# Tiles of the matmul operands at other offsets modulo 512 bytes, and gating vectors broadcast by DMA, in a two-block diffusion transformer kernel

## The chip, the cores and the metric

The kernel runs on one core of a Trainium2 chip. The metric is the device time of one execution in microseconds (us). A core has TensorE (PE, with its weight load PEld), VectorE (DVE), ScalarE (ACT), GpSimd (POOL) and SyncE (SP, which here only starts DMAs), an on-chip memory of 128 partitions (SBUF), in which a tile lies at the same address in every partition, and accumulators (PSUM) into which TensorE writes.

## The reference

The first block is two layers of a diffusion transformer on two streams of 256 tokens of 1024 columns, a main one and a context one. In short:

```python
mod = (silu_c @ lp["w_mod"] + lp["b_mod"])[:, None, :]
sh1, sc1, gt1, sh2, sc2, gt2 = jnp.split(mod, 6, axis=-1)
...
h = modulate(x, lp["g_norm1"], sh1, sc1)
proj = h @ lp["w_in"]
...
x = x + gt1 * merge_branches(o_mla, o_gqa, o_four, proj[..., GATE_START:], lp)
x = x + gt2 * conv_ffn(modulate(x, lp["g_norm2"], sh2, sc2), lp)
```

`merge_branches` adds a latent attention, a grouped attention and a Fourier mixer under sigmoid gates and multiplies by `w_o`. The context stream does the same with its own `mod` (`gt1`, `gt2` of it are used in layer 0 only). The second block takes the main stream on: swiglu feed-forward parts of 2816 columns (`ffn_wi`, `ffn_wo`), attention mixers with dilated and windowed masks (`a_wqkv`) and an embedding term (`p`). All of it is float32.

`gt1` and `gt2` are the gating vectors: 1024 numbers each, by which every token's row is multiplied. Three pairs of layer and stream use them twice each, so there are six such products.

## The kernel before, in words

**Three products for one.** Each float32 operand of a large product is split into a high half, rounded to the fast format fp32r, and a low half that holds the rest (`split`, L105 to L108: ACT casts the high half at L107, DVE subtracts at L108). `mm3` (L128 to L131) then runs three matmuls into one accumulator: high by high (L129), high by low (L130 or L131, depending on which operand stands first), low by high. A matmul has a stationary operand, 128x128, which PEld loads, and a moving operand, of 256 to 512 columns, which PE streams. The load of the next stationary tile runs beside the streaming of the present matmul. So at any time PE reads two places in the SBUF: the moving tile of one matmul, and the stationary tile of the next.

**Which is which.** Where the names read `mm<-xTh,wh`, the first is the stationary operand's tile for some groups and the moving one for others: weights move past stationary tokens in the token-major products (`L129 mm<-xTh,wh`), and tokens move past stationary weights in the others (`mm<-wh,ckv`, `mm<-wh,yh`, `mm<-wh,xTh`). In the second block each half (j = 0, 1) has 128 tokens, whose tiles `xh`, `xl` (named `x` in the trace), `oh`, `ol` and `gT` are stationary, and the weights move in stretches of 512 or 256 columns.

**Weights.** `load` (L113 to L127) fetches 512 KB into `raw` by an SP DMA and splits it into tiles `wh` and `wl` of 1024 words of 4 bytes per partition. `wsps` is a list of pools from which the pairs are taken in turn.

**Where tiles lie.** A pool gives its tiles out in the order in which they are first asked for, so a tile that nothing uses (`pads`, `pad`, `padk`, `padr`) moves all that stand behind it.

**Modulation vectors.** `w_mod` is summed on DVE chunk by chunk (512 columns) into `acc` tiles, as background pieces among the weight loads. `mod_finish` (L273 to L279) adds the partitions of up to four `acc` by PE (L277) and copies the sums to a row tile by ACT (L279). `mod_columns` (L281 to L289) turns the row into columns by four PE transposes (L287) and adds `b_mod` on DVE (L289), into `mcols`. Chunks 4, 5 are `gt1`, chunks 10, 11 are `gt2`.

**Gating vectors.** `bcast_rows` (L230 to L238) spreads 1024 columns of `mcols` over all partitions: DVE makes a diagonal tile `dg` from the identity and one column (L236, eight times), PE multiplies it with a tile of ones (L237, in plain float32, which the trace shows as two hardware matmuls each), ACT copies the accumulator with a scale, 0.5 or 1 (L238, twice), into `gtb`. It is called ahead of the product with `w_o` in `layer` (L1001) and in the feed-forward part (L1090). DVE multiplies the product by `gtb` at L1010.

A scheduler of the compiler orders each engine's instructions.

Of the kernel before, what the change touches and what calls it, by code (L numbers as in the profile page):

```python
# [11 lines left out]
ALU = mybir.AluOpType  # L12
# [24 lines left out]
FL = (1, 1)  # L37
DS = 1
TC_ARGS = dict(schedule_with_timeline_sim=True)

# [6 lines left out]
def block_kernel(ctx: ExitStack, tc: tile.TileContext, a: dict, out: bass.AP):  # L47
# [9 lines left out]
    xtp = b1.enter_context(tc.tile_pool(name="xtp", bufs=1))  # L57
    pmm = ctx.enter_context(tc.tile_pool(name="pmm", bufs=6, space=PSUM))
    ptp = ctx.enter_context(tc.tile_pool(name="ptp", bufs=2, space=PSUM))
    def mmt():  # L60
# [11 lines left out]

    st.tile([128, 112], F32, name="pads", bufs=1)
    const.tile([128, 80], F32, name="pad")
    ident = const.tile([128, 128], F32, name="ident")
    nc.sync.dma_start(out=ident, in_=a["k_ident"])
    ones = const.tile([128, 128], F32, name="ones")
    dve.memset(ones, 1.0)
# [30 lines left out]

    wsps = [wsp]  # L110
    last_load = [None]

    def load(w, k0, nk, c0, n):  # L113
        raw = wraw.tile([128, CH], F32, tag="raw", name="raw")
        last_load[0] = nc.sync.dma_start(
            out=raw[:, :nk * n].rearrange("p (k c) -> p k c", k=nk),
            in_=w[k0 * 128:(k0 + nk) * 128, c0:c0 + n].rearrange("(k p) c -> p k c", p=128),
        )
        wp = wsps[0]
        wsps.append(wsps.pop(0))  # L120
        h = wp.tile([128, CH], F32R, tag="wh", name="wh")
        lo = wp.tile([128, CH], F32R, tag="wl", name="wl")
# [57 lines left out]
    cols1.tile([128, 40], F32, name="pad1")  # L180
    xbig = [xtp.tile([128, 2 * KD * SEQ], F32R, name=f"xT{i}") for i in "hl"]
    xslot = [0]
# [46 lines left out]

    def bcast_rows(wk, cols, scale, dst):  # L230

        for half in range(2):
            p = tpt()
            for k in range(4):
                dg = wk.tile([128, 128], F32, tag="dg", name="dg", bufs=8)
                dve.tensor_scalar(dg, ident, cols[:, half * 4 + k:half * 4 + k + 1], None, op0=ALU.mult)  # L236
                pe.matmul(p[:, k * 128:(k + 1) * 128], ones, dg, start=True, stop=True)  # L237
            act.activation(dst[:, half * 512:half * 512 + 512], p, ACTF.Copy, scale=scale)  # L238

# [33 lines left out]
    def mod_finish(l, accs):  # L273

        ps = mdt()
        for i, (c, s, acc) in enumerate(accs):
            pe.matmul(ps[32 * i:32 * i + 32, :], ones[:, :32], acc, start=True, stop=True)  # L277
        row, n = accs[0][2], 32 * len(accs)
        act.copy(row[:n], ps[:n])  # L279

    def mod_columns(l, accs):  # L281

        row, n = accs[0][2], 32 * len(accs)
        p2 = mdt()
        pv = p2.rearrange("p (f c) -> p f c", f=4)
        for f in range(4):
            pe.transpose(pv[:, f, :n], row[:n, f * 128:(f + 1) * 128], ident[:n, :n])  # L287
        for i, (c, s, acc) in enumerate(accs):
            dve.tensor_tensor(mcols[l][:, c * 4:c * 4 + 4, s], pv[:, :, 32 * i], bmod[:, l, c * 4:c * 4 + 4], op=ALU.add)  # L289

# [49 lines left out]
    def small(kv, l, q):  # L340

        kv.tile([128, 24], F32, name="padk")
        r = {n: brow(kv, n, a[n][l], a[n].shape[1], q) for n in ("g_ckv", "g_cq", "g_qn_gqa", "g_kn_gqa")}
# [297 lines left out]
    def layer(l, res, qgroups, front):  # L641
# [11 lines left out]
        with ExitStack() as es:  # L653
# [345 lines left out]
            for g in qgroups:  # L999
                gtb[g] = gw_.tile([128, D], F32, tag="gtb", name="gtb")  # L1000
                bcast_rows(gw_, mcols[l][:, 16:24, 1 - g], 0.5, gtb[g])  # L1001
            x2 = new_xT(ng)
# [20 lines left out]
    def conv_ffn(l, res, xT, groups, done):  # L1023
# [6 lines left out]
        with ExitStack() as es:  # L1030
# [5 lines left out]
            for f0, f1 in parts:  # L1036
# [49 lines left out]
                if f0 == 0:  # L1086
                    flush(1 + 3 * l)
                    for g in groups:
                        gtb[g] = fw.tile([128, D], F32, tag="gtb", name="gtb")
                        bcast_rows(fw, mcols[l][:, 40:48, 1 - g], 1.0, gtb[g])  # L1090
                rate, bg_rate[0] = bg_rate[0], R3
# [86 lines left out]
    rg = ctx.enter_context(tc.tile_pool(name="rg", bufs=1))  # L1178
    rg.tile([128, 48], F32, name="padr")
    rope2 = ld(rg, "rope2", a["k_rope2"], [128, 2, 32])  # L1180
    nsink = brow(rg, "nsink", a["b_sink_2"][0], 16)
    dve.tensor_scalar(nsink, nsink, -1.0, 0.0, op0=ALU.mult, op1=ALU.add)
    loaded, gains = {}, {}
    chain = {"end": [], "n": 0}

    def w2t(name, shape=(128, 512), dt=F32):
# [24 lines left out]
    def pre_norm(j, i, n):  # L1211

        g = gain(j, i, n)
        with tc.high_priority(100):
            xT = tuple(rg.tile([128, KD, 128], F32R, tag=f"x{p}{j}", name="x") for p in "hl")
            for hf, sl in enumerate(halves()):
# [62 lines left out]
    def ffn2(j, i, n):  # L1279
# [5 lines left out]
        for c in range(6):  # L1285
# [4 lines left out]
            if c == 0:  # L1290
                t = rg.tile([128, 6144], F32R, tag=f"R{j}", name="gT")[:, :2 * FT * 128].rearrange("p (z f c) -> p z f c", z=2, f=FT)
                gT = (t[:, 0], t[:, 1])
# [35 lines left out]
    def mixer(j, i):  # L1328
# [27 lines left out]
        qT = v3(R, 4608, nqT)  # L1356
        oT = tuple(rg.tile([128, 8, 128], F32R, tag=f"o{p}{j}", name="oT") for p in "hl")

# [263 lines left out]
```

## Time and profile before

| what | value |
|---|---|
| time, median of 3 runs | 2495.92 us (2492.79 to 2496.34) |
| the profiled execution's own time | 2496.4 us |
| its span, first to last instruction | 2494.6 us |
| TensorE's mean granted clock | 0.993 of full speed |
| PE busy | 2420.9 us, 97% of the span |
| PEld, DVE, ACT, POOL busy | 2021.0, 1601.6, 1238.8, 161.1 us |

A matmul's busy time in the trace reaches into the next one's, since matmuls are pipelined. What counts for the end is the distance from one start to the next, called the pitch below, read from the timeline. Full speed of TensorE is 2.4 GHz, one column of a fast-format matmul per cycle: 512 columns take 213.3 ns, 256 take 106.7 ns, and the rest of the pitch is what is lost between two matmuls.

### The profile page before, as it was taken

The page shows a single profiled execution, that of the slowest core. Times are in us where ns is not written, and L with a number is a line of the kernel's source. Part 1 is how long each engine was busy: PE and PEld are TensorE (multiplying, and loading weights), DVE is VectorE, ACT ScalarE, POOL GpSimd, SP SyncE. Part 2 cuts the span into 40 slices and gives each one's busy share as a digit, 9 for nine tenths or more (in the row PEclk, how much of TensorE's full clock was granted, in tenths as well). Part 3 has the DMA queues.
Part 4 walks back from the last instruction along what each step waited for, and adds up shares of the span by engine and source line. Part 5 has one row for each costly group of instructions (what it writes and reads, how often), then busy time and mean ns, then how long its engine had stood idle before and what let it go on. Part 6 is the DMA issues. An engine that isn't in the chain of part 4 may idle for free.

```text
span 2494.6 us, 34647 instructions
## 1 busy us (share of the span) xinstructions
PE 2420.9 (97%) x13091; PEld 2021.0 (81%) x13091; DVE 1601.6 (64%) x2609; ACT 1238.8 (50%) x2044; POOL 161.1 (6%) x291
## 2 busy tenths in 40 slices
PE   7999999999999989999999999999999999999998
PEld 6885788788887878699899788789788788777886
DVE  4457666758877667767786555656654755666555
ACT  4567432344324346744565444556544644475444
POOL 3320000000000025000000000100000100110001
PEclk9999999999999999999999999999999999999999
DMA  7220255424454435157566665662665565525653
GB/s 264 85 64 28 78 171 162 151 82 142 136 177 135 159 97 184 42 187 236 160 182 214 189 186 185 194 186 81 194 186 195 180 187 186 193 86 176 187 186 114
DMA packets 236613, 388.32 MB, mean 156 GB/s; under 512 B 14621, under 2 KB 122045, under 8 KB 236445
## 3 DMA queue, kind: packets, MB, share of 16 engines
q1 hardware_dynamic: 235581, 384.14, 49.1%
q0 software_dynamic: 864, 1.96, 0.3%
q8 instruction: 103, 1.69, 0.3%
q14 instruction: 65, 0.53, 0.1%
HBM read 383.95 MB, written 1.05 MB: 154 GB/s over the span
## 4 chain that ended last, share of the span: by engine, by line
PE 85%; DVE 6%; ACT 3%; DMA 3%; issue 1%; POOL 1%; SPq 0%; DVEq 0%; POOLq 0%; ACTq 0%
PE mm L129 25%; PE mm L131 25%; PE mm L130 25%; DMA raw<-in_w_mod_dram 2%; PE mm L581 2%; PE mm L1423 1%; PE tp L502 1%; ACT p L596 1%; DVE acc L271 1%; DVE wl L108 1%; PE mm L1454 1%; PE tp L1323 1%; PE tp L1300 1%; PE mm L626 1%; DVE p L604 1%
## 5 line engine op out<-in xcount | busy, mean ns | idle before, releaser
L108 DVE TENSOR_TENSOR wl<-raw,wh 128x1024 fp32r<-128x1024 f32 (+2 forms) x612 | 738.7, 1211 | 490.2 <-ACT wh L107 468.2
L107 ACT CAST wh<-raw 128x1024 fp32r<-128x1024 f32 (+2 forms) x612 | 635.2, 1043 | 701.9 <-PE mm L131 470.5
L131 PE MATMUL mm<-wh,x 128*128 128x512 f32 (+1 forms) x1072 | 389.6, 371 | 1.0 <-DVE x L1225 1.0
L130 PE MATMUL mm<-wl,x 128*128 128x512 f32 (+1 forms) x1072 | 386.8, 370 | 0.0
L129 PE MATMUL mm<-wh,x 128*128 128x512 f32 (+1 forms) x1072 | 379.6, 371 | 3.9 <-ACT x L1224 3.5
L129 PE MATMUL mm<-xTh,wh 128*128 128x256 f32 (+1 forms) x1120 | 373.3, 335 | 0.0
L131 PE MATMUL mm<-xTh,wl 128*128 128x256 f32 (+1 forms) x1120 | 372.0, 332 | 0.0
L130 PE MATMUL mm<-xTl,wh 128*128 128x256 f32 (+1 forms) x1120 | 372.0, 332 | 0.0
L129 PEld LDWEIGHTS mm<-wh,x 128*128 128x128 f32 x1072 | 202.0, 189 | 38.9 <-ACT x L1224 6.5
L129 PEld LDWEIGHTS mm<-xTh,wh 128*128 128x128 f32 x1120 | 214.1, 192 | 22.9 <-issue 2.0
L131 PEld LDWEIGHTS mm<-wh,x 128*128 128x128 f32 x1072 | 201.9, 189 | 37.1 <-DVE x L1225 5.2
L131 PEld LDWEIGHTS mm<-xTh,wl 128*128 128x128 f32 x1120 | 213.9, 191 | 20.8 <-issue 0.8
L130 PEld LDWEIGHTS mm<-xTl,wh 128*128 128x128 f32 x1120 | 213.9, 191 | 19.7
L130 PEld LDWEIGHTS mm<-wl,x 128*128 128x128 f32 x1072 | 202.2, 189 | 33.2 <-DVE wl L108 0.3
L271 DVE SCALAR_TENSOR_TENSOR acc<-raw,cT,acc 128x512 f32<-128x512 f32 x224 | 160.3, 746 | 69.7 <-DMA raw<-in_w_mod_dram 68.8
L130 PE MATMUL mm<-wl,gT 128*128 128x512 f32 x352 | 134.9, 391 | 0.0
L131 PE MATMUL mm<-wh,gT 128*128 128x512 f32 x352 | 134.4, 389 | 0.0
L129 PE MATMUL mm<-wh,gT 128*128 128x512 f32 x352 | 116.1, 391 | 0.0
L129 PE MATMUL mm<-wh,gh 128*128 128x512 f32 x264 | 103.7, 394 | 3.1 <-DVE t L1137 3.1
L131 PE MATMUL mm<-wh,gl 128*128 128x512 f32 x264 | 103.6, 392 | 0.0
L130 PE MATMUL mm<-wl,gh 128*128 128x512 f32 x264 | 103.5, 392 | 0.0
L1068 ACT ACTIVATE uc<-mm,cb,cw 128x512 f32<-128x512 f32 (+1 forms) x88 | 58.7, 668 | 72.8 <-PE mm L131 69.9
(328 smaller groups left out, 3783.0 us busy)
## 6 DMA issues: line engine op xcount, KB each, us to landing
raw<-in_ffn_wi_dram SPq DMA_DIRECT2D x176, 512.0 KB, 3.7
raw<-in_w_up_dram SPq DMA_DIRECT2D x88, 512.0 KB, 3.5
raw<-in_ffn_wo_dram SPq DMA_DIRECT2D x88, 512.0 KB, 3.2
raw<-in_w_mod_dram SPq DMA_DIRECT2D x80, 512.0 KB, 4.4
raw<-in_w_in_dram SPq DMA_DIRECT2D x68, 512.0 KB, 4.4
raw<-in_w_down_dram SPq DMA_DIRECT2D x44, 512.0 KB, 4.8
raw<-in_a_wqkv_dram SPq DMA_DIRECT2D x36, 512.0 KB, 4.6
mraw<-in_w_mod_dram SPq DMA_DIRECT2D x16, 512.0 KB, 9.6
```

Source lines behind the costliest of these rows:

```text
L107: act.copy(hdst, src)
L108: dve.tensor_tensor(ldst, src, f32(hdst), op=ALU.subtract)
L129: pe.matmul(o, lhs[0], rhs[0], start=start, stop=False)
L130: pe.matmul(o, lhs[0], rhs[1], start=False, stop=False)
L131: pe.matmul(o, lhs[1], rhs[0], start=False, stop=stop)
L271: eng.scalar_tensor_tensor(acc, raw, col, acc, op0=ALU.mult, op1=ALU.add)
L502: pe.transpose(pv[:rows, i, :], blocks[i0 + i], ident)
L581: pe.matmul(v, q_of(h, qt), k_of(h), start=True, stop=True)
L596: act.activation(ps[e], ss[e], ACTF.Exp, scale=r_of(heads[0], qt)[:, e:e + 1], bias=nm[:, e:e + 1], accum_out=sm[:, e:e + 1])
L604: dve.tensor_scalar(ps[e], ps[e], rc[:, e:e + 1], None, op0=ALU.mult)
L626: pe.matmul(av[e * 64:(e + 1) * 64, :SEQ], v_of(h, kt), pts[e][:, kt, :], start=kt == 0, stop=kt == nk - 1)
L1068: act.activation(uc, p[:, :T], ACTF.Identity, scale=conv[1][:, l, f:f + 1], bias=conv["b"][:, l, f:f + 1])
```

## The change

Two things are done at once.

**Layout.** Unused tiles are put in, taken out or resized, so that operand tiles start at other offsets modulo 512 bytes. In words of 4 bytes, modulo 128:

| tile | before | after |
|---|---|---|
| `wh` | 0 | 0 |
| `wl` | 0 | 72 |
| `xTh`, `xTl` | 0, 0 | 0, 24 |
| `yh`, `yl` (what `w_o` multiplies) | 0, 0 | 24, 24 |
| `ckv`, `cq` | 24 | 24 |
| `gh`, `gl`, layer 0 | 0, 0 | 0, 0 |
| `gh`, `gl`, layer 1 | 0, 0 | 24, 24 |
| `xh0`, `xl0`, `xh1`, `xl1` | 0 | 104, 8, 72, 32 |
| `oh0`, `ol0`, `oh1`, `ol1` | 0 | 32, 80, 8, 0 |
| `gT` of j = 0, of j = 1 | 0, 0 | 48, 40 |

For two consecutive matmuls in fp32r, take the start of the second one's stationary tile less the start of the first one's moving tile, modulo 128 words: the distance of the two places that PE reads side by side. The built programs, with the same 10,554 matmuls in fp32r, count so:

| distance in words | 512 columns, before | after | 256 columns, before | after |
|---|---|---|---|---|
| 0 | 6,862 | 1,546 | 2,940 | 1,336 |
| 24 | 88 | 423 | 154 | 102 |
| other odd multiples of 8 | 0 | 2,964 | 0 | 714 |
| multiples of 16, not 0 | 0 | 2,024 | 0 | 944 |

(Other widths are not counted here. The sums differ by 7 and 2, since pairs that a gating matmul or a transpose parted now meet.)

**Gating vectors.** The chunks 4, 5, 10 and 11 go another way. Their row of sums is written to the device memory (12 POOL DMAs of 2 KB). When needed, POOL fetches the row and `b_mod`'s piece, each spread over 128 partitions by the DMA (512 KB written each, 6 + 6 DMAs), adds them (6 additions of 128x1024) and halves three of them (3 operations of 128x1024). `bcast_rows` goes, with its 48 diagonals on DVE, 48 matmuls (96 in hardware) on PE and 12 copies on ACT. `mod_columns` does nothing for a group that holds gating chunks alone, so 12 of the 36 transposes of L287 go as well.

```diff
+GATES = (4, 5, 10, 11)
...
-    st.tile([128, 112], F32, name="pads", bufs=1)
-    const.tile([128, 80], F32, name="pad")
+    st.tile([128, 40], F32, name="pads", bufs=1)
+    const.tile([128, 48], F32, name="pad")
...
         h = wp.tile([128, CH], F32R, tag="wh", name="wh")
+        if wp not in spaced:
+
+            spaced.append(wp)
+            wp.tile([128, 72], F32, name="padw", bufs=1)
         lo = wp.tile([128, CH], F32R, tag="wl", name="wl")
...
-    xbig = [xtp.tile([128, 2 * KD * SEQ], F32R, name=f"xT{i}") for i in "hl"]
+    xbig = [xtp.tile([128, 2 * KD * SEQ], F32R, name="xTh")]
+    xtp.tile([128, 24], F32, name="padx")
+    xbig.append(xtp.tile([128, 2 * KD * SEQ], F32R, name="xTl"))
...
-    def bcast_rows(wk, cols, scale, dst):
...
+    def gate_all(wk, l, c0, s, half, dst):
+
+        b = wk.tile([128, D], F32, tag="gbias", name="gbias", bufs=1)
+        pool.dma_start(out=b, in_=a["b_mod"][l, None, c0 * 512:c0 * 512 + D].to_broadcast([128, D]))
+        pool.dma_start(out=dst, in_=gate_row(l, c0, s).to_broadcast([128, D]))
+        pool.tensor_tensor(dst, dst, b, op=ALU.add)
+        if half:
+            pool.tensor_scalar(dst, dst, 0.5, 0.0, op0=ALU.mult, op1=ALU.add)
...
         act.copy(row[:n], ps[:n])
+        for i, (c, s, acc) in enumerate(accs):
+            if c in GATES:
+                at = (c % 2) * 512
+                pool.dma_start(out=gate_row(l, c - c % 2, s)[:, at:at + 512], in_=row[32 * i:32 * i + 1, :])
...
         row, n = accs[0][2], 32 * len(accs)
+        if all(c in GATES for c, _, _ in accs):
+            return
...
-        kv.tile([128, 24], F32, name="padk")
...
-                bcast_rows(gw_, mcols[l][:, 16:24, 1 - g], 0.5, gtb[g])
+                gate_all(gw_, l, 4, 1 - g, True, gtb[g])
...
-                        bcast_rows(fw, mcols[l][:, 40:48, 1 - g], 1.0, gtb[g])
+                        gate_all(fw, l, 10, 1 - g, False, gtb[g])
...
-    rg.tile([128, 48], F32, name="padr")
...
+    FRONT = dict(xh0=80, xl0=32, xh1=64, xl1=88, oh0=0, ol0=48, oh1=56, ol1=120)
+
+    def rg_tile(shape, dt, tag, name):
+        if FRONT.get(tag):
+            rg.tile([128, FRONT.pop(tag)], F32, name=f"pad{tag}")
+        return rg.tile(shape, dt, tag=tag, name=name)
...
-            xT = tuple(rg.tile([128, KD, 128], F32R, tag=f"x{p}{j}", name="x") for p in "hl")
+            xT = tuple(rg_tile([128, KD, 128], F32R, f"x{p}{j}", "x") for p in "hl")
...
-                t = rg.tile([128, 6144], F32R, tag=f"R{j}", name="gT")[:, :2 * FT * 128].rearrange("p (z f c) -> p z f c", z=2, f=FT)
+                at = (16, 8)[j]
+                t = rg.tile([128, 6144], F32R, tag=f"R{j}", name="gT")[:, at:at + 2 * FT * 128].rearrange("p (z f c) -> p z f c", z=2, f=FT)
```

**What moves.** TensorE, the product with `w_o` in layer 0 (weights `wh`, `wl` stationary, the merged branches `yh`, `yl` moving), before:

```order
L130 MATMUL mm<-wl,yh 128x512
L237 MATMUL tp<-dg,ones 128x128 x8
L131 MATMUL mm<-wh,yl 128x512
L129 MATMUL mm<-wh,yh 128x512
L130 MATMUL mm<-wl,yh 128x512
```

With the change the triples follow each other without that row, here and at the other five places; on TensorE nothing else of note changes its place.

POOL, ahead of the same product in layer 1 (`rqM` is a norm of the attention, `s` the statistics of the norm behind the product), with the change; before, the two norm rows were followed at once by the statistics:

```order
L861 TENSOR_SCALAR rqM<-rqM,rcQ 128x8
L300 DMA gate_10279<-acc 16x1x32 x2
L251 DMA gbias<-in_b_mod_dram 128x1024
L252 DMA gtb<-gate_10279 128x1024
L251 DMA gbias<-in_b_mod_dram 128x1024
L252 DMA gtb<-gate_8192 128x1024
L253 TENSOR_TENSOR gtb<-gtb,gbias 128x1024 x2
L255 TENSOR_SCALAR gtb<-gtb 128x1024
L143 TENSOR_SCALAR s_10858<-s_10856 128x1
```

Eight rows stand between the norm and the statistics now, among them both gating vectors of layer 1; the halving of the one stands behind the two additions.

VectorE at the same place, before (L108 is the subtraction of `split`, L112 after the change; L1010 multiplies by the gate, L1033 after):

```order
L236 TENSOR_SCALAR dg<-ident,mcols_99 128x128 x4
L108 TENSOR_TENSOR yl<-yacc,yh 128x256
L236 TENSOR_SCALAR dg<-ident,mcols_99 128x128 x2
L108 TENSOR_TENSOR wl<-raw,wh 128x1024
L236 TENSOR_SCALAR dg<-ident,mcols_99 128x128 x8
L108 TENSOR_TENSOR wl<-raw,wh 128x1024 x2
L1010 TENSOR_TENSOR t_10914<-mm,gtb 128x512
```

and with the change:

```order
L112 TENSOR_TENSOR wl<-raw,wh 128x1024
L112 TENSOR_TENSOR yl<-yacc,yh 128x256 x2
L112 TENSOR_TENSOR wl<-raw,wh 128x1024 x4
L1033 TENSOR_TENSOR t_10790<-mm,gtb 128x512
L1033 TENSOR_TENSOR t_10793<-mm,gtb 128x512
L112 TENSOR_TENSOR wl<-raw,wh 128x1024
```

The sixteen diagonals are gone, and one more subtraction than before stands ahead of the first product with the gate.

## Rows read from the trace of the kernel before

**Rows 1.** The page's part 1, busy time by engine, and TensorE's granted clock in 40 slices.

```profile
PE 2420.9 (97%) x13091; PEld 2021.0 (81%) x13091; DVE 1601.6 (64%) x2609; ACT 1238.8 (50%) x2044; POOL 161.1 (6%) x291
...
PEclk9999999999999999999999999999999999999999
```

**Rows 2.** The page's part 4, the chain that ended last, by engine and line.

```profile
PE 85%; DVE 6%; ACT 3%; DMA 3%; issue 1%; POOL 1%; SPq 0%; DVEq 0%; POOLq 0%; ACTq 0%
PE mm L129 25%; PE mm L131 25%; PE mm L130 25%; DMA raw<-in_w_mod_dram 2%; PE mm L581 2%; PE mm L1423 1%; PE tp L502 1%; ACT p L596 1%; DVE acc L271 1%; DVE wl L108 1%; PE mm L1454 1%; PE tp L1323 1%; PE tp L1300 1%; PE mm L626 1%; DVE p L604 1%
```

**Rows 3.** The largest group of PE by shape: count | busy us, mean ns | idle before, releaser.

```profile
L131 PE MATMUL mm<-wh,x 128*128 128x512 f32 x848 | 326.2, 393 | 1.0 <-DVE x L1225 1.0
```

**Rows 4.** Timeline of PE, distance 0, 512 columns: start us, duration, operation.

```profile
599.70 0.39 PE L129 MATMUL mm<-xTh,wh 128*128 128x512 f32 x1
...
604.46 0.39 PE L129 MATMUL mm<-xTh,wh 128*128 128x512 f32 x1
```

**Rows 5.** Timeline of PE, distance 24, 512 columns.

```profile
87.26 0.40 PE L129 MATMUL mm<-wh,ckv 128*128 128x512 f32 x1
...
90.77 0.40 PE L129 MATMUL mm<-wh,ckv 128*128 128x512 f32 x1
```

**Rows 6.** Timeline of PE, distance 0, 256 columns.

```profile
1249.81 0.28 PE L129 MATMUL mm<-xTh,wh 128*128 128x256 f32 x1
...
1252.33 0.28 PE L129 MATMUL mm<-xTh,wh 128*128 128x256 f32 x1
```

**Rows 7.** Timeline of PE, distance 24, 256 columns, two stretches.

```profile
124.18 0.28 PE L129 MATMUL mm<-wh,cq 128*128 128x256 f32 x1
...
125.98 0.28 PE L129 MATMUL mm<-wh,cq 128*128 128x256 f32 x1
...
158.71 0.28 PE L130 MATMUL mm<-wl,cq 128*128 128x256 f32 x1
...
160.11 0.28 PE L130 MATMUL mm<-wl,cq 128*128 128x256 f32 x1
```

**Rows 8.** Timeline of PE, distance 0, just behind transposes of other shapes.

```profile
139.51 0.39 PE L130 MATMUL mm<-wl,xTh 128*128 128x512 f32 x1
...
140.21 0.39 PE L130 MATMUL mm<-wl,xTh 128*128 128x512 f32 x1
140.43 0.39 PE L131 MATMUL mm<-wh,xTl 128*128 128x512 f32 x1
```

**Rows 9.** Timeline of PE, one broadcast of a gating vector.

```profile
485.04 1.95 PE L237 MATMUL tp<-dg,ones 128*128 128x128 f32 x16
486.74 0.48 PE L131 MATMUL mm<-wh,yl 128*128 128x512 f32 x1
487.05 0.39 PE L129 MATMUL mm<-wh,yh 128*128 128x512 f32 x1
```

**Rows 10.** Timeline of PE, a group of transposes of a modulation row.

```profile
668.91 0.66 PE L287 MATMUL mm<-ident,acc 128*128 128x128 f32 x4 [0.73 <-ACT acc L279]
669.32 0.47 PE L129 MATMUL mm<-wh,gh 128*128 128x512 f32 x1
```

**Rows 11.** Timeline of DVE, the product with the gate in layer 1.

```profile
1179.94 0.41 DVE L108 TENSOR_TENSOR yl<-yacc,yh 128x256 fp32r<-128x256 f32 x1
...
1188.19 1.42 DVE L1010 TENSOR_TENSOR t<-mm,gtb 128x512 f32<-128x512 f32 x2 [1.43 <-ACT gtb L238]
```

**Rows 12.** Groups of POOL: the issue of a DMA, and products of 64 and 128 columns.

```profile
L1479 POOL DMA_DIRECT2D Rp<-in_p_dram x8 | 4.4, 553 | 363.3 <-PE mm L131 356.5 <-ACT junk L1229 6.8
...
L378 POOL TENSOR_TENSOR rgq<-rtab,g_qn_gqa 128x64 f32<-128x64 f32 x4 | 1.4, 373 | 0.0
...
L378 POOL TENSOR_TENSOR rgq<-rtab,g_qn_gqa 128x128 f32<-128x128 f32 x2 | 1.0, 479 | 0.0
```

**Rows 13.** DMA issues from POOL's queue: KB each, us from issue to landing.

```profile
mask<-in_k_mask_a_dram POOLq DMA_DIRECT2D x1, 512.0 KB, 4.5
```

**Rows 14.** Who waited for the sums of L277: engine, tile, line, us and times.

```profile
  DVE acc L269: 5.3, 3
```

More of the change, by code (lines that the diff above doesn't have):

```diff
@@ L58, in block_kernel @@
     pmm = ctx.enter_context(tc.tile_pool(name="pmm", bufs=6, space=PSUM))
+    rowp = ctx.enter_context(tc.tile_pool(name="rowp", bufs=1, space=bass.MemoryType.DRAM))
     ptp = ctx.enter_context(tc.tile_pool(name="ptp", bufs=2, space=PSUM))
@@ L69, in stat @@
         return st.tile([128, n], F32, tag=f"s{n}", name=f"s{n}")
-    st.tile([128, 112], F32, name="pads", bufs=1)
-    const.tile([128, 80], F32, name="pad")
+    st.tile([128, 40], F32, name="pads", bufs=1)
+    const.tile([128, 48], F32, name="pad")
     ident = const.tile([128, 128], F32, name="ident")
     nc.sync.dma_start(out=ident, in_=a["k_ident"])
-    ones = const.tile([128, 128], F32, name="ones")
+    ones = const.tile([128, 32], F32, name="ones")
     dve.memset(ones, 1.0)
@@ L108, in split @@
         dve.tensor_tensor(ldst, src, f32(hdst), op=ALU.subtract)
-    wsps = [wsp]
+    wsps, spaced = [wsp], []
     last_load = [None]
@@ L228, in proj_tok, with gate_row @@
         token_major(ps, chunks, mms, evac, tail, skip)
-    def bcast_rows(wk, cols, scale, dst):
[L232 to L238, printed above, removed]
+    gates = {}
+    def gate_row(l, c0, s):
+        if (l, c0, s) not in gates:
+            gates[l, c0, s] = rowp.tile([1, D], F32, name=f"gate{l}{c0}{s}")
+        return gates[l, c0, s]
+    def gate_all(wk, l, c0, s, half, dst):
[5 more added lines that the diff above has]
+            pool.tensor_scalar(dst, dst, 0.5, 0.0, op0=ALU.mult, op1=ALU.add)
     mcols = [cols1.tile([128, 48, 2], F32, name=f"mcols{l}") for l in range(2)]
@@ L276, in mod_finish @@
         for i, (c, s, acc) in enumerate(accs):
-            pe.matmul(ps[32 * i:32 * i + 32, :], ones[:, :32], acc, start=True, stop=True)
+            pe.matmul(ps[32 * i:32 * i + 32, :], ones, acc, start=True, stop=True)
         row, n = accs[0][2], 32 * len(accs)
         act.copy(row[:n], ps[:n])
+        for i, (c, s, acc) in enumerate(accs):
+            if c in GATES:
+                at = (c % 2) * 512
+                pool.dma_start(out=gate_row(l, c - c % 2, s)[:, at:at + 512], in_=row[32 * i:32 * i + 1, :])
     def mod_columns(l, accs):
         row, n = accs[0][2], 32 * len(accs)
+        if all(c in GATES for c, _, _ in accs):
+            return
         p2 = mdt()
@@ L288, in mod_columns @@
         for i, (c, s, acc) in enumerate(accs):
-            dve.tensor_tensor(mcols[l][:, c * 4:c * 4 + 4, s], pv[:, :, 32 * i], bmod[:, l, c * 4:c * 4 + 4], op=ALU.add)
+            if c not in GATES:
+                dve.tensor_tensor(mcols[l][:, c * 4:c * 4 + 4, s], pv[:, :, 32 * i], bmod[:, l, c * 4:c * 4 + 4], op=ALU.add)
     def mod_pieces(l, cs, vecs):
@@ L1356, in mixer @@
         qT = v3(R, 4608, nqT)
-        oT = tuple(rg.tile([128, 8, 128], F32R, tag=f"o{p}{j}", name="oT") for p in "hl")
+        oT = tuple(rg_tile([128, 8, 128], F32R, f"o{p}{j}", "oT") for p in "hl")
         def q_evac(p, n, c0):
```

## The prediction

> **What bounds the kernel now.** The busy shares come first [rows 1]: TensorE is busy for 2420.9 of 2494.6 us and its granted clock stands at the top level, 2.4 GHz, in every slice, while VectorE, the next, has 64%. There is neither a clock that could rise nor a second engine close to its limit. The chain of waits comes second [rows 2]: 85% of it is PE, and 75% of the span are the three lines of the split product. PE waits for next to nothing there: 1.0 us over 848 matmuls in the largest group [rows 3]. So the time is the number of matmuls times the pitch, the distance from one start to the next. The mean duration of 393 ns in that row says little, since matmuls overlap; the pitch is read from starts in the timeline.
>
> At distance 0, 21 steps of 512 columns run from 599.70 to 604.46 us: 226.7 ns each [rows 4]. Of 256 columns, 21 steps run from 1249.81 to 1252.33: 120.0 each [rows 6]. At 2.4 GHz the columns alone take 213.3 and 106.7 ns, so both widths lose the same 13.3 ns between two matmuls, over some 10,000 matmuls 0.13 ms. That is what the first half of the change may touch.
>
> Three more stretches show that the 13.3 ns are no constant. `ckv` is the one moving operand of 512 columns that lies elsewhere, 24 words from the stationary tiles: 15 steps from 87.26 to 90.77 us, 234.0 ns each [rows 5]. `cq` lies at the same distance with 256 columns: 15 steps from 124.18 to 125.98 at 120.0, and later 12 steps from 158.71 to 160.11 at 116.7 [rows 7]. And just behind transposes a stretch at distance 0 is out of step: three steps of 512 columns take 0.70 us, 233 ns each, the next 0.22 [rows 8]. So the operands' place is not without effect, but the two rows at another distance point to opposite sides: dearer by 7.3 ns at 512 columns, cheaper by up to 3.3 at 256.
>
> **The change, part by part.** The sum is made against the profiled execution's own 2496.4 us, 0.5 us above the median of 2495.92. What a measurement of this kernel can tell from no change is about 0.2%, or 5 us.
>
> *Gating matmuls removed.* Of the 96 hardware matmuls of L237, sixteen start at 485.04 and the next product at 486.74 [rows 9]: 1.70 us, six times, 10.2 us. The next step of the product takes 487.05 - 486.74 = 0.31 us where 0.227 is usual: 0.08 us more at each of eight places, 0.7 us. Sum 10.9 us, all on TensorE, which is the path. The diagonals on DVE and the copies on ACT that go with them lie beside the products, covered by the lead of the weight splits; I count them at nothing, and where the lead is short their going is a gain, which I leave in the range.
>
> *Transposes removed.* Three groups of four. A group takes 669.32 - 668.91 = 0.41 us, after a wait of 0.73 where the row is late [rows 10]: 1.2 to 3.4 us for three, taken as 2.3.
>
> *Row DMAs added.* Twelve on POOL, at 553 ns for an issue [rows 12], on an engine with a load of 6%. The row lies in an `acc` tile, which the next sums overwrite; DVE already waited 5.3 us for L277 before doing so [rows 14], and now waits until the row has been read. Covered, this costs nothing; uncovered, the landing time of a transfer, 4.5 us [rows 13]. Taken as 1, since DVE has a third of its time free.
>
> *Vectors by DMA and POOL.* The nearest transfer of 512 KB from POOL's queue lands 4.5 us after its issue [rows 13]. An addition of 128x1024 I work out from products of 64 and 128 columns, 373 and 479 ns [rows 12]: 1.66 ns a column, so 479 + 896 x 1.66 = 1.97 us; a halving as much at most. The vectors of layer 0 and of the feed-forward parts are asked for early, and the time until their use covers them. The tight place is layer 1, where both vectors are added ahead of the halving. If POOL starts at 1180, when the last `yl` is under way [rows 11], four issues take 2.2 us, the last transfer 4.5, two additions 3.9, the halving 2.0: ready at 1192.6, and DVE took up the gated product at 1188.2 after a wait of 1.43 for the old vector [rows 11]. Behind that row of DVE stand the residual and the next subtraction `wl`, and the next products wait for both. If POOL starts some microseconds earlier, which the rows in memory allow, it costs nothing. Ends 0 and 1192.6 - 1188.2 = 4.4 us, taken as 2. The same section of the Trainium skill that the second rival names states a rule against this part: GpSimd shares a port pair with VectorE, under an exclusive lock. No row here shows it; an estimate from the additions and halvings would be 9 x 2.0 = 18 us of DVE held up, of which the path, with a third of DVE free, would see little.
>
> So the second half of the change is worth -10.9 - 2.3 + 1 + 2 = -10.2 us, between -10.9 - 3.4 = -14.3 and -10.9 - 1.2 + 4.5 + 4.4 = -3.2.
>
> *Layout.* By the table of distances 6,862 - 1,546, some 5,320 pairs of 512 columns, leave distance 0, and 2,940 - 1,336, some 1,600 of 256. No row shows the distances that they go to, but for 24. Bounds for 512 columns: 7.3 ns dearer, as `ckv` [rows 5], is +38.8 us if all went that way; cheaper by all the 13.3 ns that are lost now [rows 4] is -70.8 us. For 256: nothing, by the first stretch of `cq` [rows 7], and -13.3 x 1,600 = -21.3 us at the most. Between them I take the second stretch of `cq` for both widths, some 3.0 ns cheaper, as it is the longest row of a pitch below the usual one, and the one short step of 512 columns, 0.22 us [rows 8], lies about as far below 226.7: 5,320 x 3.0 = 16.0 us and 1,600 x 3.0 = 4.8 us, together -20.8. The picture behind it: at distance 0 the two readings meet in the same way at each matmul and hold a fixed step; moved apart, they meet less.
>
> The Trainium skill, "TensorE: Matmul & The Clock Gate", section "Back-to-back issue gap", gives for the step of a single matmul, without the budget of its weight load, its columns at the clock and some 2.5 ns more: 215.8 ns for 512 columns. The trace does not agree at distance 0, where it is 226.7 with the loads beside it [rows 4]; were the difference the layout's doing alone, the estimate from that page would be a gain of 5,320 x 10.9 = 58 us.
>
> Sum of the forecast: 2496.4 - 10.2 - 20.8 = **2465.4 us**. Its own range goes from 2425, where two thirds of the bound on 512 and 256 columns come back (-61) with the gates, to 2482, where the layout gives 4 us.
>
> **The rivals.**
>
> *The layout does nothing.* Then 13.3 ns are what a load beside a stream costs wherever the tiles lie, and only the gates count: 2496.4 - 10.2 = 2486.2, between 2482 and 2493. For it speaks the first stretch of `cq`, 120.0 at distance 24 as at 0 [rows 6, 7]; against it, the second stretch and `ckv` [rows 5, 7]. The Trainium skill, "SBUF — State Buffer", section "Who interferes with whom", says that TensorE has two independent read ports, one for the moving operand and one for weight loads. By that rule the layout would do nothing and this rival would hold; the trace does not bear it out for the two readings of TensorE itself, which differ by 7.3 ns between distances 0 and 24.
>
> *The layout makes it slower.* What `ckv` shows is then the rule at 512 columns for any distance at which the readings fall out of step, and the 233 ns of the stretch that was out of step at distance 0 [rows 8] are the same thing. Its place are the products of the second block, whose stationary tiles all move, and the pair of `xTl` and `wl` in the first. The new pairs at odd multiples of 8, 423 + 2,964 - 88 = 3,299, give +24.1 us at 7.3 ns each, all moved ones +38.8. With the gates: 2496.4 - 10.2 + 24.1 = **2510.3**, up to 2525. It decides from a mean rise of 10.2 / 5,320 = 1.9 ns a pair. For it speaks that 512 columns are most of the work and that both rows out of step are dearer there; against it, that the new distances lie mostly at 40 to 104 words, which no row shows, and that 256 columns at 24 are not dearer.
>
> *The gating vectors come late* is inside the bounds: 4.4 us at layer 1, which turns no sign by itself.
>
> **How the numbers follow.** The forecast has 0.44, the layout without effect 0.25, the slower layout 0.31. The forecast is faster by over 5 us throughout. The second case lies between 2482 and 2493, nearly all of it faster (0.21), the rest within 5 us (0.04). The third runs from a rise that the gates cover (faster 0.02, same 0.04) to one that they don't (0.25). Together faster 0.67, same 0.08, slower 0.25. The range, 2436 to 2510, leaves out some 0.06 below, where more than half of the lost 13.3 ns would come back, and some 0.13 above, the dearer half of the third case.
>
> **What would show it.** PE's count falls by 108 matmuls (96 and 12); POOL's busy time grows by about 9 x 2.0 + 24 x 0.55 = 31 us. The verdict on the layout is in the starts: steps of 512 columns near 224 (forecast), still 226.7 (no effect), or near 234 (slower). `xT` moves one pair in three, `xTl` to `wl`, and so should change little; the tokens of the second block (`x`, `gT`) move nearly all pairs and should change most. Between 1180 and 1195 us a wait of DVE for POOL's `gtb` would show late vectors. The forecast is wrong if the steps of `x` and `gT` keep 226.7, or if some distances gain what others lose.

## The result, and the profile after

The changed kernel takes 2510.16 us (median of 4 runs, 2507.77 to 2516.23) beside 2496.13 for the kernel before (4 runs): a ratio of 1.0063, 95% interval 1.0051 to 1.0075. It is slower by some 14 us. The forecast was 2465.4; the time is that of the second rival, the layout that makes it slower (2510.3).

One thing in the text ahead has to be put right first. The trace names the moving operand of a matmul first and the stationary one second, always: in `mm<-wh,ckv` and `mm<-wh,yh` the weights move past stationary tokens, in `mm<-xTh,wh` the tokens move past stationary weights. The sections before the prediction have it the wrong way round in the first block (and the prediction calls `ckv` moving). The distances of the table were counted with the right roles, so the numbers stand. And where the prediction's part on the vectors points at the second rival for two read ports, it is the first, the layout that does nothing.

The page of the changed kernel, parts 1 and 4, answers to [rows 1, 2]:

```profile
PE 2434.8 (97%) x12983; PEld 2001.5 (80%) x12983; DVE 1601.7 (64%) x2549; ACT 1233.3 (49%) x2032; POOL 195.5 (8%) x324
...
PE 86%; DVE 5%; ACT 3%; DMA 3%; issue 1%; POOL 1%; SPq 0%; DVEq 0%; POOLq 0%; ACTq 0%
PE mm L137 26%; PE mm L139 26%; PE mm L138 26%; PE mm L604 1%; PE mm L1453 1%; ACT p L619 1%; PE tp L525 1%; DMA raw<-in_w_mod_dram 1%; PE mm L1484 1%; PE tp L1353 1%; PE tp L1330 1%; DVE wl L112 1%; PE mm L649 1%; DVE p L627 1%; DMA raw<-in_w_in_dram 1%
```

TensorE has 108 matmuls fewer (13,091 to 12,983) and is busy for 14 us longer. POOL has 34 us more, 31 were forecast; ACT has 5.5 us less; DVE is where it was although 48 diagonals went (five other operations took longer, see the last section); and the share of the split product's three lines in the chain has grown from 75% to 78%. So the time was lost inside TensorE, step by step.

The timeline of PE, the products of layer 0 with `xT` at 512 columns (start us, duration, operation), answers to [rows 4]:

```profile
604.27 0.40 PE L137 MATMUL mm<-xTh,wh 128*128 128x512 f32 x1
...
609.14 0.39 PE L137 MATMUL mm<-xTh,wh 128*128 128x512 f32 x1
```

21 steps in 4.87 us are 231.9 ns each, where they were 226.7. This is the group of which the prediction said that it should change little, since only one pair in three had left distance 0. All groups did the same. The table has the mean step of consecutive fp32r matmuls, from all starts in the profiled execution (steps of over 300 ns at 512 columns and over 180 at 256, which hold a pause or a lower clock, left out):

| steps | before | after |
|---|---|---|
| 512 columns, all (6,791 and 6,811) | 227.3 ns | 232.4 ns |
| 512 columns, pairs at distance 0 | 227.2 (6,712) | 232.2 (1,525) |
| 512 columns, pairs at another distance | 233.8 (79) | 232.5 (5,286) |
| 256 columns, all (3,023 and 3,016) | 119.8 | 117.9 |

Summed over all steps, pauses included and gating and transposes apart, the 7,079 steps of 512 columns took 1645.4 us before and 1676.1 after, the 3,138 steps of 256 columns 383.3 and 379.2, those of 288 and 384 columns 56.5 and 55.1, and all other work of TensorE (gating, transposes, attention) 390.4 and 378.5: +30.7 - 4.1 - 1.4 - 11.9 = +13.3, against 12.9 us of difference in the span.

The gating half did what it says. The product with `w_o` in layer 0 runs on where [rows 9] had 1.7 us of L237:

```profile
485.11 0.39 PE L138 MATMUL mm<-wl,yh 128*128 128x512 f32 x1
485.34 0.39 PE L139 MATMUL mm<-wh,yl 128*128 128x512 f32 x1
485.57 0.39 PE L137 MATMUL mm<-wh,yh 128*128 128x512 f32 x1
```

In layer 1 the vector comes late, as feared. The timeline of POOL, then that of DVE (the brackets hold the idle time before and what ended it), answer to [rows 11]:

```profile
1185.62 2.39 POOL L253 TENSOR_TENSOR gtb<-gtb,gbias 128x1024 f32<-128x1024 f32 x1 [6.59 <-DMA gtb<-gate]
1188.96 2.40 POOL L253 TENSOR_TENSOR gtb<-gtb,gbias 128x1024 f32<-128x1024 f32 x1 [0.95 <-DMA gtb<-gate]
1191.46 1.06 POOL L255 TENSOR_SCALAR gtb<-gtb 128x1024 f32<-128x1024 f32 x1
```

```profile
1192.55 1.29 DVE L1033 TENSOR_TENSOR t<-mm,gtb 128x512 f32<-128x512 f32 x2 [3.45 <-POOL gtb L255]
```

The vector was ready at 1192.5 us, by chance the very time of the prediction's working (1192.6): POOL began earlier, but a broadcast took 5.8 to 10.3 us from issue to landing where 4.5 was assumed, and an addition 2.40 where 1.97 was.

### The profile page after: what moved, and what is told of

Its sections match the earlier page's. It is cut to its first block, busy times and chain, and to the rows that moved or that the text cites. A ratio compares the mean times of both kernels' runs of the same rounds, so it can differ in the third digit from the quotient of the medians.

```text
span 2507.5 us, 34443 instructions
## 1 busy us (share of the span) xinstructions
PE 2434.8 (97%) x12983; PEld 2001.5 (80%) x12983; DVE 1601.7 (64%) x2549; ACT 1233.3 (49%) x2032; POOL 195.5 (8%) x324
## 4 chain that ended last, share of the span: by engine, by line
PE 86%; DVE 5%; ACT 3%; DMA 3%; issue 1%; POOL 1%; SPq 0%; DVEq 0%; POOLq 0%; ACTq 0%
PE mm L137 26%; PE mm L139 26%; PE mm L138 26%; PE mm L604 1%; PE mm L1453 1%; ACT p L619 1%; PE tp L525 1%; DMA raw<-in_w_mod_dram 1%; PE mm L1484 1%; PE tp L1353 1%; PE tp L1330 1%; DVE wl L112 1%; PE mm L649 1%; DVE p L627 1%; DMA raw<-in_w_in_dram 1%
## 5 line engine op out<-in xcount | busy, mean ns | idle before, releaser
L112 DVE TENSOR_TENSOR wl<-raw,wh 128x1024 fp32r<-128x1024 f32 (+2 forms) x612 | 741.1, 1215 | 506.7 <-ACT wh L111 484.8
L139 PE MATMUL mm<-wh,x 128*128 128x512 f32 (+1 forms) x1072 | 393.3, 374 | 1.0 <-DVE x L1254 1.0
L137 PE MATMUL mm<-wh,x 128*128 128x512 f32 (+1 forms) x1072 | 384.3, 375 | 3.9 <-ACT x L1253 3.5
L137 PE MATMUL mm<-wh,gT 128*128 128x512 f32 x352 | 117.9, 396 | 0.0
L137 PE MATMUL mm<-wh,xTh 128*128 128x512 f32 (+3 forms) x272 | 92.1, 343 | 4.0 <-DVE xTh L184 3.5
```

The source lines that it names most:

```text
L112: dve.tensor_tensor(ldst, src, f32(hdst), op=ALU.subtract)
L137: pe.matmul(o, lhs[0], rhs[0], start=start, stop=False)
L139: pe.matmul(o, lhs[1], rhs[0], start=False, stop=stop)
```

## The experiments

The theory after this result, **A**: the 226.7 ns are a fixed step that consecutive matmuls hold while their operands' starts agree modulo some unit; a tile that does not agree takes whole products out of step, the pairs at distance 0 in them too, and out of step 512 columns cost some 5 ns more and 256 columns some 2 less. Rivals are told with each run. All edits are to the kernel before, if not said otherwise.

**e1_gates and e2_layout: the two halves by themselves.** e1 has the diff's gating part alone and keeps the paddings of before. e2 is the rest of the diff, with

```diff
-    FRONT = dict(xh0=80, xl0=32, xh1=64, xl1=88, oh0=0, ol0=48, oh1=56, ol1=120)
+    FRONT = dict(xh0=80, xl0=32, xh1=64, xl1=88, oh0=0, ol0=48, oh1=56, ol1=112)
```

Expected of e1:

> The gating part alone, every operand tile at the offset it had before. Theory A (the loss comes from the layout: matmuls that kept a fixed step fall out of step, whatever the gating part does): the steps of 512 columns stay at 226.7 ns, PE's count falls by 108, and the time falls by about 10 us, to 2486 (2482 to 2492). Rival B (the loss comes from the gating part: its 512 KB broadcasts and POOL additions hold up loads or DVE): 2505 to 2515, with steps still at 226.7 and waits of PE at the product with w_o or behind the weight splits.

Expected of e2:

> The layout part alone, the gating vectors made by TensorE as before (one padding 8 words smaller, for room: gT at 40 and 32 words in place of 48 and 40, ol of j=1 at 120 in place of 0). Theory A: the means per width are those of the changed kernel, about 232 to 234 ns at 512 columns and 120 to 121 at 256, and the time is 2520 to 2524, about 25 us above the kernel before. Rival B: about 2496, the time of before.

e1 took 2487.66 us (6 runs) beside 2494.54 (15 runs): 0.997, interval 0.9959 to 0.9982; the spans of the two profiled executions, 2483.8 and 2494.6, are 10.8 apart. e2 took 2519.46 (4 runs): 1.0094, interval 1.0077 to 1.0111. The steps of 512 columns are 227.3 ns on average in e1 and 232.3 in e2. Those of 256 are 117.9 in e2, not the 120 to 121 expected: there A as told above goes by the measured steps. In e2's timeline the products of layer 0 with `xT` take 21 steps in 4.88 us, 232.4 ns each:

```profile
610.19 0.39 PE L132 MATMUL mm<-xTh,wh 128*128 128x512 f32 x1
...
615.07 0.40 PE L132 MATMUL mm<-xTh,wh 128*128 128x512 f32 x1
```

In e1's timeline the same products hold the old step, 21 of it in 4.76 us:

```profile
599.70 0.39 PE L133 MATMUL mm<-xTh,wl 128*128 128x512 f32 x1
...
604.46 0.39 PE L133 MATMUL mm<-xTh,wl 128*128 128x512 f32 x1
```

So the gating part is a gain of 6.9 us by the medians and the layout part a loss of 24.9; together +18 would be expected and +14 was measured, which the spread of the runs (some 4 us either way) doesn't tell apart. Rival B is out.

**e3_shift24: agreement or grid.** Is it a start on the 512-byte grid that counts, or that the operands of a product agree?

```diff
-    const.tile([128, 80], F32, name="pad")
+    const.tile([128, 104], F32, name="pad")
...
-        kv.tile([128, 24], F32, name="padk")
```

> The kernel before with one padding 24 words larger ahead of all pools, so that nearly all operand tiles (wh, wl, xT, y, o, x, gT and, by leaving out one padding, ckv and cq too) start 24 words past the 512-byte grid, at distance 0 from each other; gh and gl of layer 0 stay on the grid and are at distance 104 from the weights. Theory A1 (what counts is that the operands of a product agree modulo 512 bytes, not where they lie): steps of 226.7 ns at 512 columns everywhere but with gh of layer 0, there 231 to 234; ckv, 234 before, falls to 226.7; the time is 2496 +3 us for the gh of layer 0. Rival A2 (a start on the 512-byte grid is what counts): all steps of 512 columns go to 231 to 234, the time rises to about 2525 to 2530.

It took 2499.84 us (8 runs): 1.0016, interval 1.0006 to 1.0027, some 5 us more; A1 had 3. The timeline of PE has both cases side by side. `xTh` and `wh`, both 24 words off the grid, hold the step (21 in 4.76 us, 226.7 ns); `gh`, on the grid while `wh` is not, doesn't (21 in 4.90 us, 233.3):

```profile
599.75 0.39 PE L129 MATMUL mm<-xTh,wh 128*128 128x512 f32 x1
...
604.51 0.39 PE L129 MATMUL mm<-xTh,wh 128*128 128x512 f32 x1
...
689.86 0.39 PE L129 MATMUL mm<-wh,gh 128*128 128x512 f32 x1
...
694.76 0.39 PE L129 MATMUL mm<-wh,gh 128*128 128x512 f32 x1
```

Over the whole execution the 6,277 steps at distance 0 average 227.3 ns and the 513 at distance 104, `gh`'s, 233.4. `ckv`, now at distance 0, has a median step of 228 where it was 234; being cut up by transposes, it doesn't fall quite to 227: behind one of the interruptions its steps are 235, 229, 232 and 231 ns and only then 227, so matmuls that agree come back into step after some four others. So the difference counts, not the place. That 5 us and not 3 came is within the interval, which is 1.5 to 6.7 us.

**e4_wl64, e5_wl32, e7_wl8: how far off.** The weights' low halves alone are moved, by 64, 32 or 8 words; `K` below is that number, and two other paddings are resized so that nothing else moves modulo 512 bytes.

```diff
         h = wp.tile([128, CH], F32R, tag="wh", name="wh")
+        if wp not in spaced:
+            spaced.append(wp)
+            wp.tile([128, K], F32, name="padw", bufs=1)
         lo = wp.tile([128, CH], F32R, tag="wl", name="wl")
```

> The kernel before with the weights' low halves alone 64 words (256 bytes) further, everything else at its offset: of three pairs one is at distance 64, two stay at distance 0. Theory A1 in its strict form (any difference within a product drops all of its steps out of step): about 232 ns mean at 512 columns also for the pairs that are still at distance 0, the time 2520 to 2530. Rival A3 (each pair pays by its own distance alone): the pairs at distance 0 keep 226.7 and the time rises by at most 2,328 x 7 ns = 16 us. Rival A4 (only differences that are no multiple of some coarser unit, such as 64 words, break the step): 226.7 everywhere and 2496.

> The kernel before with the weights' low halves 32 words (128 bytes) further, everything else as it was: distances 0, 32 and 96. At 64 words the step of 226.7 ns was kept. Theory A4 with a unit of 32 words or less: 226.7 ns at 512 columns, 120.0 at 256, the time of before. Rival, a unit of 64 words: 231 to 235 ns in all products whose triples hold a low half of the weights, also at their pairs at distance 0, and about 2525 us.

> The same with 8 words (32 bytes): distances 0, 8 and 120, the size of step by which the changed kernel's offsets differ. If one tile off the unit takes whole products out of step: 231 to 235 ns at 512 columns, also at the two pairs of three that stay at distance 0, 117 to 121 at 256, and about 2520 to 2530 us, more than the 2519 of the layout part, in which every third pair or more is off too. Rival, each pair by its own distance: pairs at distance 0 keep 226.7, at most 2,328 pairs x 7 ns = 16 us more, 2511. Rival, small offsets do not matter: the time of before.

One execution each, beside medians of before of 2494.54 (e4) and 2495.61 (e5, e7):

| run | us | 512 columns, distance 0 | 512 columns, other distance | 256 columns, all |
|---|---|---|---|---|
| e4_wl64 | 2494.55 | 227.1 ns | 227.6 ns | 119.8 ns |
| e5_wl32 | 2515.25 | 230.5 | 232.3 | 118.8 |
| e7_wl8 | 2524.53 | 230.8 | 235.2 | 118.2 |

The same products of layer 0 with `xT`, in the timelines of e4, e5 and e7 in this order, 21 steps each (4.76, 4.85 and 4.90 us, so 226.7, 231.0 and 233.3 ns):

```profile
600.03 0.39 PE L132 MATMUL mm<-xTh,wh 128*128 128x512 f32 x1
...
604.79 0.39 PE L132 MATMUL mm<-xTh,wh 128*128 128x512 f32 x1
```

```profile
609.93 0.39 PE L132 MATMUL mm<-xTh,wh 128*128 128x512 f32 x1
...
614.78 0.39 PE L132 MATMUL mm<-xTh,wh 128*128 128x512 f32 x1
```

```profile
610.30 0.40 PE L132 MATMUL mm<-xTh,wh 128*128 128x512 f32 x1
...
615.20 0.40 PE L132 MATMUL mm<-xTh,wh 128*128 128x512 f32 x1
```

At 64 words (256 bytes) nothing happens (2,260 steps at distance 64 average 227.4 ns, the rest of that column is `ckv`): A1 in its strict form falls, and so do A3 and the rival that prices each pair alone, since from 32 words down the two pairs of three that stay at distance 0 are dearer too (230.5 and 230.8 for 227.2). One kind of tile, 8 words off, cost 29 us in its one execution, as much as all offsets of the change together (24.9 by the median of e2, 28 by its slowest execution). That a pair's own distance also has a part is seen in e7, where the pairs that moved are dearer than those that did not (235.2 and 230.8). For 512 columns a unit of 32 words or less is out as well; e5's loss, 20 us, is smaller than the rival's 29.

**e10_round64: the cause undone inside the changed kernel.** Its paddings are rounded so that the tiles are still apart, but by 0 or 64 words.

```diff
-    st.tile([128, 40], F32, name="pads", bufs=1)
+    st.tile([128, 48], F32, name="pads", bufs=1)
...
-            wp.tile([128, 72], F32, name="padw", bufs=1)
+            wp.tile([128, 64], F32, name="padw", bufs=1)
...
-    xtp.tile([128, 24], F32, name="padx")
+    xtp.tile([128, 64], F32, name="padx")
...
+            if l == 0:
+                gp.tile([128, 24], F32, name="padg")
...
-    FRONT = dict(xh0=80, xl0=32, xh1=64, xl1=88, oh0=0, ol0=48, oh1=56, ol1=120)
+    FRONT = dict(xh0=48, xl0=64, xh1=64, xl1=64, oh0=0, ol0=64, oh1=0, ol1=64)
...
-                at = (16, 8)[j]
+                at = (64, 0)[j]
```

> The changed kernel with its paddings rounded so that every operand tile lies at 0 or 64 words past the 512-byte grid (one padding of 24 words added ahead of gh in layer 0): the tiles are still apart, 3,974 pairs of 512 columns at distance 64 and 3,105 at 0, no other distance. Theory A with the unit of 64 words: all steps of 512 columns, ckv's too, are back at 226.7 ns and those of 256 at 120.0; the time is that of the gating part alone, 2487 (2483 to 2490). Rival (64 words kept the step only because two of three pairs stayed at 0): 231 to 235 ns in most products and 2505 to 2512.

It took 2488.21 us (5 runs) beside 2496.59 (9 runs): 0.9964, interval 0.995 to 0.9977, the gain of the gating part alone. The 3,770 steps at distance 64 average 227.4 ns and the 3,028 at distance 0 227.1. The timeline of the same products:

```profile
599.67 0.39 PE L138 MATMUL mm<-xTl,wh 128*128 128x512 f32 x1
...
604.43 0.39 PE L138 MATMUL mm<-xTl,wh 128*128 128x512 f32 x1
```

21 steps in 4.76 us. More than half of the pairs lie at distance 64 here, so it isn't that a majority at 0 holds the step: the whole loss of the change hangs on its offsets not being multiples of 64 words of each other.

**e8_mixed: out of step where it gains.** 256 columns were cheaper after the change. On top of e1, the tokens of the feed-forward part of layer 1 alone are moved:

```diff
-        at = xslot[0] * KD * SEQ
+        at = xslot[0] * (KD * SEQ - 24)
```

> The gating part with the offsets of before (2487.7 alone), and one tile moved: the tokens of the feed-forward part of layer 1, xT, start 24 words ahead, so that its 1,056 matmuls of 256 columns are at distance 24, as cq's are; all products of 512 columns stay on the grid. Theory A (out of step costs at 512 columns and gains at 256): steps of 117 to 118.5 ns in place of 120 there, 1.5 to 3 us less than the gating part alone, about 2485. Rival (256 columns gain nothing by it, as the first stretch of cq at 120.0): 2488.

2484.90 us (5 runs) beside 2495.61: 0.996, interval 0.9947 to 0.9974. The steps of that part average 118.7 ns (1,040 of them, those over 180 left out) where e1 has 120.0 (1,029): 1.3 ns or 1.4 us in all, just short of what A expected (117 to 118.5 ns, 1.5 to 3 us) and not the rival's nothing. In its timeline 21 of these steps take 2.49 us, where [rows 6] had 2.52:

```profile
1249.81 0.28 PE L133 MATMUL mm<-xTh,wl 128*128 128x256 f32 x1
...
1252.30 0.28 PE L133 MATMUL mm<-xTh,wl 128*128 128x256 f32 x1
```

The 2.8 us between the times of e8 and e1, which ran beside other executions of before, are within the intervals. In other mixtures the same steps are cheaper still: 117.8 in the changed kernel, 118.3 in e7.

**e9_fused and e11_gates_fused: the late vector.** The factor 0.5 goes to VectorE, which multiplies anyway. e9 is e8 with this, e11 is e1 with this.

```diff
-        if half:
-            pool.tensor_scalar(dst, dst, 0.5, 0.0, op0=ALU.mult, op1=ALU.add)
...
-                    dve.tensor_tensor(t, p, gtb[g][:, hf * 512:hf * 512 + 512], op=ALU.mult)
+                    dve.scalar_tensor_tensor(t, p, 0.5, gtb[g][:, hf * 512:hf * 512 + 512], op0=ALU.mult, op1=ALU.mult)
```

> The same, with the factor 0.5 of the attention gate moved from POOL into VectorE's product with the gate (a scalar_tensor_tensor in place of a tensor_tensor), so that three POOL operations go, one of which stood between the additions and VectorE's wait in layer 1. If the wait of 3.45 us of VectorE for POOL there reaches TensorE (the transposes behind it waited 3 us longer than before): 2 to 3 us less than the run before this one, 2482 to 2483. Rival (the wait is covered): no difference.

> The gating part with the offsets of before and the factor 0.5 moved to VectorE, without the moved xT. If the fused factor alone made the last gain, 2483 to 2485, as with the moved xT (2483.1); if the moved xT had a part in it, 2486 to 2488.

e9 took 2483.10 us (5 runs, 2476.02 to 2485.97), 0.995 with an interval of 0.9936 to 0.9963; e11 2484.83 (5 runs), 0.996 with 0.9948 to 0.9973. The wait of VectorE in e9 is shorter, its timeline shows:

```profile
1185.32 1.29 DVE L1024 SCALAR_TENSOR_TENSOR t<-mm,gtb 128x512 f32<-128x512 f32 x2 [2.29 <-POOL gtb L245]
```

And so is the wait of TensorE for the transposes behind it. The groups of PE by line (busy us, mean ns | idle before, releasers), of the kernel before, of e1 and of e9:

```profile
L171 PE MATMUL tp<-ident,xn 128*128 128x128 f32 x80 | 13.7, 312 | 10.0 <-ACT xg L174 5.3 <-DVE xn L164 4.7
```

```profile
L173 PE MATMUL tp<-ident,xn 128*128 128x128 f32 x80 | 14.0, 319 | 11.7 <-DVE xn L166 7.7 <-ACT xg L176 3.9
```

```profile
L173 PE MATMUL tp<-ident,xn 128*128 128x128 f32 x80 | 14.0, 320 | 9.4 <-DVE xn L166 5.6 <-ACT xg L176 3.8
```

The idle time that VectorE's `xn` ends is 4.7, 7.7 and 5.6 us: 3.0 more with the late vector, and 2.1 less with the fused factor. All the idle time before these transposes is 10.0, 11.7 and 9.4 us, since the waits for ScalarE's `xg` became shorter; so the late vector costs TensorE 1.7 us net, and the fused factor gives 2.3 back. In the times this doesn't stand out (1.8 us between e8 and e9, 2.8 between e1 and e11, both within the intervals). e11's median lies in the first of its two expected stretches, but its executions go from 2483.21 to 2490.41 us, so it does not decide whether the moved `xT` had a part. e9 has the lowest time, clear of the kernel before and of the changed one; against e8, e10 and e11 its order is not shown.

## Why the prediction was wrong, point by point

**The bound was right.** TensorE set the time, and the change showed in its steps.

**The gating matmuls and transposes** were put at -13.2 us. All work of TensorE outside the fp32r products fell by 11.9 in the changed kernel and by 10.4 in e1 (390.4 to 380.0), the longer waits for the transposes included.

**Row DMAs and late vectors** were put at +3. The late vector cost TensorE 1.7 us net in e1 (3.0 in the waits that VectorE ends, less shorter ones for ScalarE) where 2 was taken; it stands at the place that was named, within its ends of 0 and 4.4. For the row DMAs no wait stands out. The second half of the change as a whole measured -6.9 by the medians (interval -10 to -4.5) and -10.8 by the spans of the profiled executions, where -10.2 was taken, with bounds of -14.3 and -3.2: this step held.

**The layout is the step that failed**: "Between them I take the second stretch of `cq` for both widths, some 3.0 ns cheaper", -20.8 us. It measured +24.9 (e2). For 512 columns the sign was wrong. Two rows at that width were out of step, `ckv` and the stretch behind transposes [rows 5, 8], and both were dearer; the value was taken from a row of 256 columns [rows 7], the other width, because it was the only one to be cheaper. The one short step of 512 columns that it leaned on, 0.22 us [rows 8], belongs to a stretch whose nine steps average 231 ns. The picture put behind it, that two readings meet in the same way at distance 0 and meet less when moved apart, was not shown by any row. The runs show the contrary at 512 columns: the fixed step of 226.7 ns is the cheap state, and out of it steps average 231 to 235. For 256 columns the sign was right and the size about right, by two errors that cancel: 1.9 ns over all 3,016 steps (5.7 us) where 3.0 over 1,600 was taken (4.8).

**The second rival was right in its time, and its working only by luck.** It priced 3,299 pairs at odd multiples of 8 words with 7.3 ns, 24.1 us. In truth nearly all 6,800 steps paid some 5.1 ns (34.7 us; pauses shrank by 4), the pairs at distance 0 as much as the others (232.2 and 232.5), and 256 columns gave some 4 us back. What to count was not pairs but products that hold any tile out of agreement: after the change that is every one of them.

**The two rules of the Trainium skill.** The Trainium skill, page "TensorE: Matmul & The Clock Gate", section "Back-to-back issue gap", gives 215.8 ns at 512 columns for a matmul without its weight load. No run here has a mean step below 227 over its matmuls of that width, with a weight load beside each, in or out of step. By the Trainium skill, page "SBUF — State Buffer", section "Who interferes with whom", two independent read ports would make the layout neutral. The runs e4 and e7, which differ by 56 words of padding ahead of one tile and by 30 us, don't bear that out.

**VectorE held up by POOL** was put at an estimate of 18 us, little of it on the path, without a row. It measured 7.9 us in the changed kernel (rows in the last section), and among TensorE's longest waits there is none for the tiles of these operations (`wl`, `acc`, `res`).

**What stays open.** Why operands that agree modulo 64 words hold a fixed step, and why it is the cheaper one at 512 columns but not at 256, is not settled; between 32 and 64 words no other offset was tried by itself, and none of the runs separates the next matmul's weight load from the present matmul's own pair of reads. That accesses of other engines make the difference was not tested either; against it speaks that in e7 the same three steps, 233, 239 and 228 ns, repeat triple by triple through the whole stretch shown. And agreement modulo 64 words is not what holds the step at every width. The first stretch of `cq` held 120.0 ns at distance 24 [rows 7]. In the first product of layer 0 in the kernel before, the weights come in slices of 288 columns, two to a tile, so that every second slice starts at word 288, 32 words past a multiple of 64; its steps hold all the same, 45 of them in 6.00 us, 133.3 ns each, the same 13.3 above the columns:

```profile
45.27 0.30 PE L129 MATMUL mm<-wh,xTh 128*128 128x288 f32 x1
...
51.27 0.29 PE L129 MATMUL mm<-wh,xTh 128*128 128x288 f32 x1
```

So the unit of 64 words is shown for 512 columns alone.

## What to carry to other kernels

When matmuls with a weight load each follow one another, read their steps from starts, width by width: a step that repeats to the nanosecond is a state that can be lost, and a change of addresses is priced by the rows out of that state at the same width, not by those of another. Before tiles are moved apart, move one tile in one run and read the steps of all products that use it; here paddings in multiples of 64 words were free and 8 words ahead of one tile cost 29 us. Work taken off the bounding engine (here 10 us of TensorE's time in e1) is worth having by itself; measured together with a second change it can't be seen.

## What was not expected of the hardware

The offset between two operands' starts changes the time of a matmul, and at 512 columns only its value modulo 64 words (256 bytes) showed: with all tiles apart by 0 or 64 words steps of 512 columns average 227.3 ns, with one tile 8 words off 232.3. A shift of nearly all tiles by the same 24 words changed nothing (227.3 at distance 0). And the effect spreads along the product: pairs whose own operands agree go from 227.2 to 230.5 or more as soon as a third of their neighbours don't. A DMA from POOL's queue that spreads 4 KB over 128 partitions landed 5.8 to 10.3 us after its issue, as the view of that line (L252) in the trace of the changed kernel says of its six:

```profile
DMA to landing us min/median/max: 5.8/8.2/10.3
```

where the mask, 512 KB too, took 4.5 [rows 13]; and POOL's addition of 128x1024 took 2.40 us, a fifth more than the line through its smaller products gave.

While POOL adds, VectorE's work on SBUF tiles waits. In the timeline of VectorE of the changed kernel, a subtraction that begins beside POOL's addition of 1185.62 us (2.39 us long) ends 1.1 us after it; the one before takes what they all take:

```profile
1184.19 1.22 DVE L112 TENSOR_TENSOR wl<-raw,wh 128x1024 fp32r<-128x1024 f32 x1 [1.56 <-ACT wh L111]
1186.93 2.17 DVE L112 TENSOR_TENSOR wl<-raw,wh 128x1024 fp32r<-128x1024 f32 x1 [1.52 <-ACT wh L111]
```

Of the 588 subtractions of this shape two took over 1.23 us, both begun during one of POOL's additions; in the kernel before none did. With three sums and products on other tiles, all five operations that began during an addition took 2.1 to 2.9 us where 0.5 to 1.2 is usual, 7.9 us more in all, and each ended 0.3 to 1.1 us after POOL's addition. It went the other way too: a halving took 1.06 us alone and 1.91 beside a subtraction.

And the gating matmuls may have done something else on TensorE. Ahead of the feed-forward part of layer 1 TensorE waits for a norm, and its granted clock falls to 1.2 GHz, half of full speed (0.50 from 1204 to 1212 us in the kernel before, from 1192 to 1200 in e1). Before the change L237 ran at the end of that gap; without it more of the products that follow start at the low clock. In the six kernels that have L237, 1 to 12 of these steps ran at the low clock, in the six without it 14 to 25; that it is L237's absence is argued from the place, no run isolates it. The view by stretches (from and to in us, length, busy time and count of PE, granted clock, DMA share, GB/s), of the kernel before around 1211.7, where those products begin:

```profile
1212.00:1218.00 6.00, 6.00 (x48) 0.91 0.00 0
```

and of e1 around 1199.9, where they begin there:

```profile
1200.00:1206.00 6.00, 6.00 (x29) 0.52 0.03 12
```

29 matmuls in 6 us in place of 48: 25 steps of 256 columns take 213 ns there, 4 did before. In the same place of layer 0 it went the other way (4 such steps for 23), so over both places it came to nothing, 29 steps in e1 for 27 before.
